# A decoder layer on one core: six raw panel buffers from the output projection on, and additions that read PSUM banks first at the end of a sweep's seven-product part

## The chip, the cores and the metric

The kernel runs on one core of one Trainium2 chip. The metric is the device time of one execution in microseconds (us); the median of several runs counts. TensorE (PE in the profile) multiplies, VectorE (DVE) and ScalarE (ACT) do elementwise work, GpSimd (POOL) builds some tables, and SyncE (SP) issues nearly all loads, in the order of its queue.

## The reference

One decoder layer over 256 tokens of width 2048, in float32 (`D_FF` is 8192). The first part mixes tokens (a causal pooling mixer beside RWKV-7 time mixing) and gives `mix`. The change touches what follows from `w_out` on, and the memory of the mixer's tables:

```python
mix = concatenate([pool_out, rwkv_out], -1)
x = x + mix @ w_out
h2 = rms_norm(x, mlp_norm)
x = x + square(relu(h2 @ w_ffn_up)) @ w_ffn_down
gate = sigmoid(rms_norm(x, ple_norm) @ w_ple_gate)
x = x + gate * (p @ w_ple_proj)
return rms_norm(x, final_norm)
```

## The kernel before

**Split operands.** Every float32 weight is used as the sum of a high half (`wh`, rounded to the matmul's type, made by ScalarE) and a low half (`wl`, the difference, made by VectorE). A product is three matmuls: high by high, low weight by high, high by low. Each matmul has 512 moving columns and one 128 by 128 stationary tile.

**Panels and rings.** Weights come from HBM in raw panels of 128 partitions by 1024 floats (512 KB), with one SP load each (`load_raw`, L146 to L149). Raw panels, `wh` and `wl` each have a ring of three buffers in the pool `wp`. A load can be issued when the last reader of the buffer's old panel is done, `wl` mostly.

**From the output projection on.** The half of `w_out`'s rows that the mixer leaves over is done at L1138 to L1140, in four column blocks of four panels each. The feed-forward network then runs in two halves. `ffn_half` computes 4096 hidden columns with `gemm_wide` (64 panels a half; lines L1102 and L1107 are its matmuls, L157 and L158 its splits) and then adds them back into the residual stream `xr` in two *down sweeps*, one for each 1024 output columns (`down_sweep`, `pair` 0 and 1).

**A down sweep** goes over 16 row blocks `kp`, of two raw panels each (`rx`, `ry`, tile `raw_d` in the profile). A plain row block has 8 products (24 matmuls). A row block in `SEVEN` uses Strassen's way with seven products (21 matmuls); VectorE forms four sums of raw panels for it (`td`, L1257 to L1260) and there are three `wl` for it instead of two. Matmuls stand at L1217 to L1219, the splits of the sweep at L1228 and L1229; `wl_d_7b` is the low half of the second panel of row block 7. In a seven-product row block the suffixes b, c and d are `ry` and the two pairs of sums, and `wad` is the split of half of `rx` (L1254). The halves with suffix d live in a pair of buffers of their own, tag `graw`.

**Banks.** Four banks take the plain products (`d_b`), two double banks `w16` and `w57` (`d_w`) take products 1, 6 and 5, 7. After the last row block of `seven` the four banks `b1`, `b6`, `b5`, `b7` are added into `xr` (L1273 to L1282): `add` is a VectorE instruction at L1237, `u` (tile `ud`) holds b1 + b6 and then also b7. The double banks have two buffers in all, which the next user waits for: the next sweep, the next half's `gemm_wide`, or the transposes `h3t` at L1124. The four plain banks are added at the end (L1285 to L1287).

**The last sweep** of the second half has only four seven-product row blocks, loads and splits eight panels of the gate's weights beside its own (`keep`, L1156 to L1165, also with buffers of tag `graw`), and starts transposing `xr` for the gate (`between`, `h3_part`). The gate and the projection of the per-layer embeddings follow, then the final norm.

**Order.** PE's order is written out by hand up to L1080. From there on, the order on every engine and of SP's queue is made by the framework's scheduler: it goes by program order, moved forward by the number in `tc.high_priority(...)` (20000 for splits, 30000 for the plain banks' additions), and by when it expects operands to be ready. On the chip each engine keeps that order.

**Memory.** The pools `const`, `wp` and `act` last for the whole kernel. The mixer's pool `rp` is closed at L1081 (`rctx.close()`), and `fp` takes its room. In the kernel before, the tables that only the mixer reads lie in `const`.

Of the kernel before, what the change touches and what calls it, by code (L numbers as in the profile page):

```python
# [9 lines left out]
F32 = mybir.dt.float32  # L10
F32R = mybir.dt.float32r
AF = mybir.ActivationFunctionType
ALU = mybir.AluOpType
# [3 lines left out]
T = 256  # L17
# [23 lines left out]
def trunk(  # L41
# [19 lines left out]
    nc = tc.nc  # L61
# [3 lines left out]
    act = ctx.enter_context(tc.tile_pool(name="act", bufs=1))  # L65
    psm = ctx.enter_context(tc.tile_pool(name="psm", bufs=4, space=PSUM))
    rctx = ctx.enter_context(ExitStack())
    psr = rctx.enter_context(tc.tile_pool(name="psr", bufs=4, space=PSUM))

    def mm_bank(name):  # L70
# [22 lines left out]
    nc.vector.memset(eps_g, GN_EPS)  # L93
    ident = const.tile([128, 128], F32, name="ident")
    make_identity(nc, ident)
    ones = const.tile([128, 128], F32, name="ones")
    nc.vector.memset(ones, 1.0)
    jsum = const.tile([128, 128], F32, name="jsum")
    cmask = const.tile([128, 128], F32, name="cmask")
    rmask = const.tile([128, T], F32, name="rmask")  # L100
    sbd = [const.tile([128, 4, 128], F32, name=f"sbd{i}") for i in range(2)]
    nc.gpsimd.memset(cmask, 0.0)
    for r0 in (0, 64):
        nc.gpsimd.memset(cmask[r0 : r0 + 64, r0 : r0 + 64], 1.0)
    nc.gpsimd.tensor_copy(jsum, cmask)
    cen = const.tile([128, 128], F32, name="cen")
    jhead = const.tile([128, 32], F32, name="jhead")
    nc.gpsimd.memset(jhead, 0.0)
    nc.gpsimd.tensor_copy(jhead[:, 0:2], cmask[:, ::64])
    for r0 in (0, 64):  # L110
# [3 lines left out]
    nc.gpsimd.memset(rmask.rearrange("p (c t) -> p c t", t=64)[:, :, 0:1], 0.0)  # L114
    for i in range(2):
        nc.vector.memset(sbd[i], 0.0)
    edge = const.tile([128, 4, 16], F32, name="edge")
# [6 lines left out]
    wband = const.tile([128, 4, 272], F32, name="wband")  # L124

    def make_bands():
        for g, win in enumerate(WINDOWS):
# [9 lines left out]
    omu = const.tile([128, m1 - m0], F32, name="omu")  # L137
    oka = const.tile([128, 8], F32, name="oka")

    def derived():  # L140
        ka0 = PARAM_COLS["k_a"]
# [1 line left out]
        nc.vector.tensor_scalar(oka, par_sb[:, ka0 : ka0 + 8], -1.0, 1.0, op0=ALU.mult, op1=ALU.add)  # L143
        nc.vector.scalar_tensor_tensor(cen, jsum, -1.0 / 64.0, ident, op0=ALU.mult, op1=ALU.add)

    def load_raw(src, n, name):  # L146
        raw = wp.tile([128, 1024], F32, tag="raw", name=f"raw_{name}")
        nc.sync.dma_start(raw[:, 0:n], src)
        return raw  # L149

# [166 lines left out]
    hsel = const.tile([128, 4, 128], F32R, name="hsel")  # L317
    nc.gpsimd.tensor_copy(hsel, hsel_f)

    def flat(t_):  # L320
# [122 lines left out]
    zf = const.tile([128, 3, T], F32, name="zf")  # L443
    zwa, zg, zg2 = zf[:, 0], zf[:, 1], zf[0:64, 2]

    def wag_out():
# [688 lines left out]
        return part, lambda k: hl[:, :, k, :]  # L1135

    h2_part, h2 = transposed("h2")
    for n in range(4):  # L1138
        run(gemm_toks(w_out[n], mix, f"o{n}", lambda banks: residual(banks, n), (6, 7, 2, 3)))
        h2_part("mlp_norm", n)  # L1140
# [54 lines left out]
    def down_sweep(hf, pair, ys, sboxes, hooks=(), between=None, seven=SEVEN):  # L1195

        nm = f"d{hf}{pair}"
        hooks = dict(hooks)
        b2, b4, b3, bx = (mm_bank(f"{nm}_b{i}") for i in range(4))
        w16, w57 = (wide_bank(f"{nm}_w{i}") for i in range(2))  # L1200
        b1, b6, b5, b7 = w16[:, 0], w16[:, 1], w57[:, 0], w57[:, 1]
        todo = {"2": 0, "3": 0, "4": 0, "x": 0, "1": 0, "5": 0, "6": 0, "7": 0}
        banks = {"2": b2, "3": b3, "4": b4, "x": bx, "1": b1, "5": b5, "6": b6, "7": b7}
        for kp in range(16):
            if kp in seven:
                for n in "1234567":
                    todo[n] += 1
            else:
                for n in "234x":
                    todo[n] += 2  # L1210
        left = dict(todo)

        def prod(n, a_, w_):
            first, last = left[n] == todo[n], left[n] == 1
            left[n] -= 1
            (ah, al), (wh, wl) = a_, w_
            nc.tensor.matmul(banks[n], ah, wh, start=first, stop=False)  # L1217
            nc.tensor.matmul(banks[n], ah, wl, start=False, stop=False)  # L1218
            nc.tensor.matmul(banks[n], al, wh, start=False, stop=last)  # L1219

        def halves_of(src, name, own=False):

            pool, kw = (fp, dict(bufs=2)) if own else (wp, {})
            wh = pool.tile([128, 1024], F32R, tag="graw" if own else "wh", name=f"wh_{name}", **kw)
            wl = pool.tile([128, 1024], F32R, tag="graw" if own else "wl", name=f"wl_{name}", **kw)
            with tc.high_priority(20000):
                for c in range(2):
                    nc.scalar.activation(wh[:, c * 512 : c * 512 + 512], src[:, c * 512 : c * 512 + 512], AF.Copy)  # L1228
                nc.vector.tensor_tensor(wl, src, wh.bitcast(F32), op=ALU.subtract)  # L1229
            return [(wh[:, c * 512 : c * 512 + 512], wl[:, c * 512 : c * 512 + 512]) for c in range(2)]  # L1230

        def xs(tt, c):
            o = pair * 1024 + c * 512
            return xr[tt][:, o : o + 512]

        def add(tt, c, src):
            nc.vector.scalar_tensor_tensor(xs(tt, c), src, s2[:, tt : tt + 1], xs(tt, c), op0=ALU.mult, op1=ALU.add)  # L1237

        for q, kp in enumerate((0, 2, 1, 4, 3, *range(5, 16)) if pair else range(16)):
            if q in hooks:  # L1240
                hooks[q]()
            y, j = ys[kp // 2], kp % 2 * 512
            a11, a21, a12, a22 = ((y[:, j + i * 128 : j + i * 128 + 128], y[:, 1024 + j + i * 128 : 1152 + j + i * 128]) for i in range(4))
            rx, ry = (load_raw(w_down[pair, hf * 32 + 2 * kp + i], 1024, f"{nm}_{kp}_{i}") for i in range(2))
            if kp in seven:
                i = SEVEN.index(kp)
                st = sboxes[kp][:, i % 2 * 1024 : i % 2 * 1024 + 1024]
                s1, s2_, s3, s4 = ((st[:, c * 128 : c * 128 + 128], st[:, 512 + c * 128 : 640 + c * 128]) for c in range(4))
                t_ = a8(1, f"t{nm}_{kp}")
                t1, t3, t2, t4 = (t_[:, c * 512 : c * 512 + 512] for c in range(4))  # L1250
                wa = fp.tile([128, 1024], F32R, tag="wa", name=f"wa{nm}_{kp}")
                w11 = wa[:, 0:512], wa[:, 512:1024]
                with tc.high_priority(20000):
                    split_sb(*w11, rx[:, 0:512])  # L1254
                w21, w22 = halves_of(ry, f"{nm}_{kp}b")
                with tc.high_priority(20000):
                    nc.vector.tensor_tensor(t1, rx[:, 512:1024], rx[:, 0:512], op=ALU.subtract)  # L1257
                    nc.vector.tensor_tensor(t3, ry[:, 512:1024], rx[:, 512:1024], op=ALU.subtract)
                    nc.vector.tensor_tensor(t2, t3, rx[:, 0:512], op=ALU.add)
# [12 lines left out]
            if kp == seven[-1]:  # L1272
                add(0, 0, b1)  # L1273
                u = fp.tile([128, 512], F32, tag="r", bufs=2, name=f"u{nm}")
                nc.scalar.activation(u, b1, AF.Copy)
                nc.vector.tensor_tensor(u, b6, u, op=ALU.add)
                add(0, 1, u)
                add(0, 1, b5)
                nc.vector.tensor_tensor(u, b7, u, op=ALU.add)
                add(1, 0, u)  # L1280
                add(1, 1, u)
                add(1, 1, b5)  # L1282
                if between is not None:
                    between()
        for n, tt, c in (("2", 0, 0), ("4", 1, 0), ("3", 0, 1), ("x", 1, 1)):  # L1285
            with tc.high_priority(30000):
                add(tt, c, banks[n])  # L1287
# [184 lines left out]
```

## Time and profile before

| what | value |
|---|---|
| median of three runs | 1193.17 us (1190.15 to 1196.21) |
| the profiled execution, its own time | 1191.21 us |
| its span | 1189.5 us |
| PE busy | 1169.6 us, 98% |
| DVE busy | 859.2 us, 72% |
| ACT busy | 702.5 us, 59% |
| DMA | 216.81 MB, mean 182 GB/s |
| granted clock of TensorE, mean | 0.998 |

The span is what the trace covers; the execution's own time is a little longer. All durations of single instructions below come from this one execution. In a row of the trace the first number is the start in us, the second the duration, then the engine, the line, the operation, and output and inputs by tile name; in brackets stands how long the engine was idle before it and what ended that. In a row of waits stand the total in us, the number of times and the longest.

### The profile page before, as it was taken

The numbers are of one execution on the slowest core, as the hardware profiler recorded it, in microseconds if no ns is written. First come the engines' busy times: TensorE is split into PE (matmuls) and PEld (weight loads), VectorE is DVE, ScalarE is ACT, GpSimd is POOL, SyncE is SP. The second block draws the span as 40 slices with busy tenths as digits, with TensorE's granted clock in tenths as the row PEclk, the third lists the DMA queues.
The fourth block names the chain that finished last, engine by engine and source line by source line (L and its number), as shares of the span: only waits on it lengthen the run. The fifth ranks groups of instructions, "written<-read, shape, count | busy, mean of one in ns | idle before, by whom it ended". The sixth has DMA issues, their size and how long they took to land.

```text
span 1189.5 us, 17244 instructions
## 1 busy us (share of the span) xinstructions
PE 1169.6 (98%) x6428; PEld 974.0 (82%) x6428; DVE 859.2 (72%) x1156; ACT 702.5 (59%) x1302; POOL 14.0 (1%) x73
## 2 busy tenths in 40 slices
PE   9999999999999999999999999999999999999997
PEld 8787777788887888888878788888888888778886
DVE  7696996955666666667778888666678788787543
ACT  8777858676445565545555564555555555568544
POOL 2100000000000000000000000000000000000000
PEclk9999999999999999999999999999999999999999
DMA  8454443354455565566556566655555665776631
GB/s 291 158 193 143 142 142 108 118 184 154 140 180 172 181 194 187 187 193 193 181 193 197 193 207 207 192 192 190 184 193 190 200 203 188 272 245 221 206 107 71
DMA packets 60756, 216.81 MB, mean 182 GB/s; under 512 B 6784, under 2 KB 7552, under 8 KB 60288
## 3 DMA queue, kind: packets, MB, share of 16 engines
q1 hardware_dynamic: 60240, 215.12, 55.0%
q8 instruction: 50, 0.82, 0.3%
q10 hardware_dynamic: 432, 0.60, 0.1%
q14 instruction: 34, 0.28, 0.1%
HBM read 213.59 MB, written 2.10 MB: 181 GB/s over the span
## 4 chain that ended last, share of the span: by engine, by line
PE 83%; DMA 6%; DVE 5%; ACT 3%; issue 2%; SPq 0%; POOL 0%; ACTq 0%; POOLq 0%; DVEq 0%
PE u_w L1102 20%; PE u_w L1107 10%; PE d_b L1218 5%; PE d_b L1219 5%; PE d_b L1217 4%; DMA raw_d<-in_w_ffn_down_dram 4%; PE gt_b L228 2%; PE gt_b L231 2%; PE gt_b L232 2%; PE zk_b L231 1%; PE zk_b L232 1%; PE o_b L231 1%; PE o_b L232 1%; PE zv_b L228 1%; PE o_b L228 1%
## 5 line engine op out<-in xcount | busy, mean ns | idle before, releaser
L1102 PE MATMUL u_w<-h,wh_u 128*128 128x512 f32 x1024 | 321.9, 395 | 0.0
L157 ACT ACTIVATE wh_u<-raw_u 128x512 fp32r<-128x512 f32 x256 | 147.5, 623 | 164.2 <-PE u_w L1102 101.6
L158 DVE TENSOR_TENSOR wl_u<-raw_u,wh_u 128x1024 fp32r<-128x1024 f32 x128 | 156.5, 1224 | 113.3 <-ACT wh_u L157 111.7
L1107 PEld LDWEIGHTS u_w<-h,wl_u 128*128 128x128 f32 x1024 | 192.3, 188 | 45.4
L1107 PE MATMUL u_w<-h,wl_u 128*128 128x256 f32 x1024 | 201.4, 278 | 0.0
L1102 PEld LDWEIGHTS u_w<-h,wh_u 128*128 128x128 f32 x1024 | 156.0, 189 | 0.1
L158 DVE TENSOR_TENSOR wl_gt<-raw_gt,wh_gt 128x1024 fp32r<-128x1024 f32 x24 | 29.4, 1224 | 24.1 <-ACT wh_gt L157 24.0
L157 ACT ACTIVATE wh_gt<-raw_gt 128x512 fp32r<-128x512 f32 x48 | 28.0, 641 | 22.8 <-PE gt_b L232 17.2
L1257 DVE TENSOR_TENSOR td<-raw_d 128x512 f32<-128x512 f32 x22 | 15.2, 692 | 32.6 <-DMA raw_d<-in_w_ffn_down_dram 32.6
L231 PE MATMUL gt_b<-wh_gt,h 128*128 128x512 f32 x96 | 37.3, 389 | 0.0
L232 PE MATMUL gt_b<-wh_gt,h 128*128 128x512 f32 x96 | 37.3, 389 | 0.0
L162 ACT ACTIVATE wad<-raw_d 128x512 fp32r<-128x512 f32 x22 | 13.9, 632 | 36.6 <-DMA raw_d<-in_w_ffn_down_dram 36.4
L158 DVE TENSOR_TENSOR wl_o<-raw_o,wh_o 128x1024 fp32r<-128x1024 f32 x16 | 19.6, 1223 | 12.9 <-ACT wh_o L157 11.4
L157 ACT ACTIVATE wh_o<-raw_o 128x512 fp32r<-128x512 f32 x32 | 18.4, 623 | 16.3 <-issue 6.9
L157 ACT ACTIVATE wh_zp<-raw_zp 128x512 fp32r<-128x512 f32 x32 | 18.6, 623 | 15.9 <-PE zp_b L232 7.2
L158 DVE TENSOR_TENSOR wl_zk<-raw_zk,wh_zk 128x1024 fp32r<-128x1024 f32 x16 | 19.4, 1222 | 9.9 <-ACT wh_zk L157 9.9
L231 PE MATMUL zv_b<-wh_zv,hTh 128*128 128x512 f32 x64 | 26.0, 406 | 0.0
L231 PE MATMUL zk_b<-wh_zk,hTh 128*128 128x512 f32 x64 | 25.2, 394 | 0.7 <-ACT wh_zk L157 0.7
L231 PE MATMUL zp_b<-wh_zp,hTh 128*128 128x512 f32 x64 | 25.7, 401 | 0.0
L228 PE MATMUL gt_b<-wl_gt,h 128*128 128x512 f32 x96 | 25.7, 389 | 0.0
L157 ACT ACTIVATE wh_zk<-raw_zk 128x512 fp32r<-128x512 f32 x32 | 18.4, 624 | 11.9 <-DMA raw_zk<-in_w_in_dram 5.7
L231 PE MATMUL zr_b<-wh_zr,hTh 128*128 128x512 f32 x64 | 25.4, 397 | 0.0
(809 smaller groups left out, 2966.1 us busy)
## 6 DMA issues: line engine op xcount, KB each, us to landing
raw_u<-in_w_ffn_up_dram SPq DMA_DIRECT2D x128, 512.0 KB, 3.5
raw_d<-in_w_ffn_down_dram SPq DMA_DIRECT2D x128, 512.0 KB, 4.2
raw_gt<-in_w_ple_gate_dram SPq DMA_DIRECT2D x24, 512.0 KB, 3.5
raw_zk<-in_w_in_dram SPq DMA_DIRECT2D x16, 512.0 KB, 3.8
raw_zr<-in_w_in_dram SPq DMA_DIRECT2D x16, 512.0 KB, 3.3
raw_zv<-in_w_in_dram SPq DMA_DIRECT2D x16, 512.0 KB, 3.4
raw_zp<-in_w_in_dram SPq DMA_DIRECT2D x16, 512.0 KB, 3.3
raw_o<-in_w_out_dram SPq DMA_DIRECT2D x16, 512.0 KB, 3.6
```

The lines of the kernel that those rows point to most:

```text
L157: nc.scalar.activation(wh[:, a * 512 : (a + 1) * 512], raw[:, a * 512 : (a + 1) * 512], AF.Copy)
L158: nc.vector.tensor_tensor(wl, raw, wh.bitcast(F32), op=ALU.subtract)
L162: nc.scalar.activation(h_ap, src_ap, AF.Copy)
L228: nc.tensor.matmul(banks[tt], ah[:, ts_], halves[a][1], start=False, stop=last)
L231: nc.tensor.matmul(banks[tt], ah[:, ts_], halves[a][0], start=i + a == 0, stop=False)
L232: nc.tensor.matmul(banks[tt], al[:, ts_], halves[a][0], start=False, stop=False)
L1102: nc.tensor.matmul(bank[:, ct, :].rearrange("p (s t) -> p s t", s=2), wh[:, cs[ct]], hl, start=k == 0, stop=False, skip_group_check=True,)
L1107: nc.tensor.matmul(bank[:, ct, 0:T], wl[:, cs[ct]], hl[:, 0, :], start=False, stop=k == 15, skip_group_check=True)
L1217: nc.tensor.matmul(banks[n], ah, wh, start=first, stop=False)
L1218: nc.tensor.matmul(banks[n], ah, wl, start=False, stop=False)
L1219: nc.tensor.matmul(banks[n], al, wh, start=False, stop=last)
L1257: nc.vector.tensor_tensor(t1, rx[:, 512:1024], rx[:, 0:512], op=ALU.subtract)
```

## The change

Two things are changed, and a third makes room for the first.

1. From the first `w_out` panel of L1138 on, `load_raw` counts its panels. From the fifth on, three panels in turn take buffers of a new ring of three in `fp` (tag `raw2`), and the next three take the old ring in `wp`. Each buffer is so used again after six panels.
2. In the additions after the seven-product part, the order is changed: `b5` is added to both places before `u` is. All instructions up to the last read of a bank are put at the splits' priority (20000); the last two, which read only `u`, stay at program order.
3. Tables that only the mixer reads (`ones`, `jsum`, `cmask`, `rmask`, `sbd`, `cen`, `jhead`, `edge`, `wband`, `omu`, `oka`, `hsel`, `zf`) move from `const` to a pool `mixc` that closes with the mixer.

```diff
+    mixc = rctx.enter_context(tc.tile_pool(name="mixc", bufs=1))
...
-    ones = const.tile([128, 128], F32, name="ones")
+    ones = mixc.tile([128, 128], F32, name="ones")
...
+    deep = []
+
     def load_raw(src, n, name):
-        raw = wp.tile([128, 1024], F32, tag="raw", name=f"raw_{name}")
+        own = False
+        if deep:
+            deep.append(name)
+            own = len(deep) > 5 and len(deep) % 6 < 3
+        if own:
+            raw = fp.tile([128, 1024], F32, tag="raw2", bufs=3, name=f"raw_{name}")
+        else:
+            raw = wp.tile([128, 1024], F32, tag="raw", name=f"raw_{name}")
         nc.sync.dma_start(raw[:, 0:n], src)
         return raw
...
     h2_part, h2 = transposed("h2")
+    deep.append("w_out")
     for n in range(4):
...
             if kp == seven[-1]:
-                add(0, 0, b1)
                 u = fp.tile([128, 512], F32, tag="r", bufs=2, name=f"u{nm}")
-                nc.scalar.activation(u, b1, AF.Copy)
-                nc.vector.tensor_tensor(u, b6, u, op=ALU.add)
-                add(0, 1, u)
-                add(0, 1, b5)
-                nc.vector.tensor_tensor(u, b7, u, op=ALU.add)
+                with tc.high_priority(20000):
+                    add(0, 0, b1)
+                    nc.scalar.activation(u, b1, AF.Copy)
+                    nc.vector.tensor_tensor(u, b6, u, op=ALU.add)
+                    add(0, 1, b5)
+                    add(1, 1, b5)
+                    add(0, 1, u)
+                    nc.vector.tensor_tensor(u, b7, u, op=ALU.add)
                 add(1, 0, u)
                 add(1, 1, u)
-                add(1, 1, b5)
                 if between is not None:
                     between()
```

More of the change, by code (lines that the diff above doesn't have):

```diff
@@ L95, in trunk @@
     make_identity(nc, ident)
-    ones = const.tile([128, 128], F32, name="ones")
+    ones = mixc.tile([128, 128], F32, name="ones")
     nc.vector.memset(ones, 1.0)
[L98 to L101, printed above, removed]
+    jsum = mixc.tile([128, 128], F32, name="jsum")
+    cmask = mixc.tile([128, 128], F32, name="cmask")
+    rmask = mixc.tile([128, T], F32, name="rmask")
+    sbd = [mixc.tile([128, 4, 128], F32, name=f"sbd{i}") for i in range(2)]
     nc.gpsimd.memset(cmask, 0.0)
@@ L105, in trunk @@
     nc.gpsimd.tensor_copy(jsum, cmask)
-    cen = const.tile([128, 128], F32, name="cen")
-    jhead = const.tile([128, 32], F32, name="jhead")
+    cen = mixc.tile([128, 128], F32, name="cen")
+    jhead = mixc.tile([128, 32], F32, name="jhead")
     nc.gpsimd.memset(jhead, 0.0)
@@ L116, in trunk @@
         nc.vector.memset(sbd[i], 0.0)
-    edge = const.tile([128, 4, 16], F32, name="edge")
+    edge = mixc.tile([128, 4, 16], F32, name="edge")
     nc.vector.memset(edge, 1.0)
@@ L121, in trunk @@
             nc.gpsimd.memset(edge[:, g, t : t + 1], float(win) / (t + 1))
-    wband = const.tile([128, 4, 272], F32, name="wband")
+    wband = mixc.tile([128, 4, 272], F32, name="wband")
     def make_bands():
@@ L136, in trunk @@
     m0, m1 = PARAM_COLS["mu_r"], PARAM_COLS["mu_wag"] + 3
-    omu = const.tile([128, m1 - m0], F32, name="omu")
-    oka = const.tile([128, 8], F32, name="oka")
+    omu = mixc.tile([128, m1 - m0], F32, name="omu")
+    oka = mixc.tile([128, 8], F32, name="oka")
     def derived():
@@ L316, in trunk @@
     nc.gpsimd.affine_select(hsel_f, hsel_f, [[-2048, 4], [-1, 128]], ALU.is_ge, 0.0, base=63, channel_multiplier=64)
-    hsel = const.tile([128, 4, 128], F32R, name="hsel")
+    hsel = mixc.tile([128, 4, 128], F32R, name="hsel")
     nc.gpsimd.tensor_copy(hsel, hsel_f)
@@ L441, in head_norm @@
         nc.vector.reciprocal(rs1, rs1)
-    zf = const.tile([128, 3, T], F32, name="zf")
+    zf = mixc.tile([128, 3, T], F32, name="zf")
     zwa, zg, zg2 = zf[:, 0], zf[:, 1], zf[0:64, 2]
```

## The prediction

> **What bounds the kernel now.** I read the page's engine rows first, which have TensorE (PE) busy nearly always, then a table of stretches for where it is not, then PE's waits, and only then single instructions. The table gives the length of each stretch, each engine's busy time in it, the granted clock and the DMA share.
>
> ```profile
> core 0: us, PE busy (x) PEld busy (x) DVE busy (x) ACT busy (x) POOL busy (x), PEclk, DMA share, GB/s
> ...
> 557.60:727.60 170.00, 168.19 (x735) 136.49 (x734) 141.67 (x160) 94.59 (x167) 0.00 (x0) 1.00 0.61 196
> 727.60:905.90 178.30, 178.30 (x1025) 155.54 (x1024) 119.67 (x145) 92.56 (x165) 0.00 (x0) 1.00 0.59 191
> 905.90:1080.20 174.30, 171.68 (x761) 139.69 (x759) 145.59 (x164) 103.66 (x186) 0.00 (x0) 1.00 0.67 222
> ```
>
> The reader is to see that in the second half's up-projection (727 to 905; the first half's is alike) PE is busy for every microsecond: deeper raw buffers can give nothing there. In the two stretches of down sweeps (557 to 727, 905 to 1080) PE has gaps. Everything the change can win lies in these 344 us. How much is that? A busy PE row hides part of a stall, because matmul ends are modelled, so I count by the spacing of starts.
>
> ```profile
> 690.81 0.39 PE L1217 MATMUL d_b<-wh_d_9a,y 128*128 128x512 f32 x1
> ...
> 696.25 0.39 PE L1217 MATMUL d_b<-wh_d_10a,y 128*128 128x512 f32 x1
> ...
> 682.81 0.39 PE L1217 MATMUL d_b<-wh_d_7b,y 128*128 128x512 f32 x1
> 683.40 0.50 PE L1218 MATMUL d_b<-wl_d_7b,y 128*128 128x512 f32 x1 [0.20 <-DVE wl_d_7b L1229]
> 683.73 0.40 PE L1219 MATMUL d_b<-wh_d_7b,y 128*128 128x512 f32 x1
> ...
> 1057.61 0.66 PE L1124 MATMUL h3t<-ident,x 128*128 128x128 f32 x4 [0.27 <-DVE ud L1276]
> 1058.02 0.48 PE L1219 MATMUL d_b<-wh_d_12a,y 128*128 128x512 f32 x1
> ```
>
> Panel row 9 is 24 matmuls in 696.25 − 690.81 = 5.44 us: 0.2267 us each without a stall. A sweep with six seven-product rows is 10 × 24 + 6 × 21 = 366 matmuls, the last sweep, with four, 12 × 24 + 4 × 21 = 372. The first pair would take 732 × 0.2267 = 165.9 us and takes 170.0: 4.1 lost. The second would take 738 × 0.2267 = 167.3 plus about twenty transposes at 0.41 / 4 each (2.1, from 1057.61 to 1058.02), and takes 174.3: 4.9 lost. So **9.0 us is the ceiling** of the whole change, 0.75% of the time. The Trainium skill, page "TensorE: Matmul & The Clock Gate", section "Wait — 56ns, not 53.3ns?", gives 215.7 ns as the warm start-to-start time for 512 columns; by it 1470 matmuls would hide another 16 us of loss in the sweeps. This trace shows 0.2267 in runs without any wait, so its spacing decides, and that 16 us is not there to win.
>
> The rows of 682.81 to 683.73 show what one stall costs: the next starts come 0.59 and 0.33 us later instead of 0.2267 each, 0.46 lost where the bracket says 0.20. A stall costs its idle time and 0.26 us. PE's other waits in the sweeps are these, beside the 0.27 of the h3t row at 1057.61:
>
> ```profile
> PE d_b L1218 <- DVE wl_d_8b L1229: 0.9, 1, 0.9
> PE h3t L1124 <- DVE x L1237: 0.7, 1, 0.7
> PE d_w L1218 <- DVE wl_d_6d L1229: 0.7, 1, 0.7
> PE d_b L1218 <- DVE wl_d_7b L1229: 0.6, 2, 0.4
> PE d_b L1218 <- DVE wl_d_6b L1229: 0.5, 1, 0.5
> PE d_b L1218 <- DVE wl_d_12b L1229: 0.3, 1, 0.3
> PE d_w L1218 <- DVE wl_d_6c L1229: 0.2, 1, 0.2
> PE d_b L1217 <- DVE x L1237: 0.2, 1, 0.2
> ```
>
> Seven stalls wait for a low half (wl) on DVE, three for additions. The chain of waits says why wl is late, for one of them:
>
> ```profile
> 590.04 4.28 DMA raw_d<-in_w_ffn_down_dram
> ...
> 594.96 1.15 ACT wh_d_7b L1228 x2
> ...
> 596.13 1.24 DVE wl_d_7b L1229
> ...
> 597.41 0.50 PE d_b L1218
> ```
>
> A raw panel must land (4.28), be rounded (1.15) and subtracted (1.24): 597.37 − 590.04 = 7.3 us with the gaps between. Only when its last reader is done does the buffer take the next load. Three buffers so give one panel per 2.4 us, with nothing to spare: PE eats two panels in 21 × 0.2267 or 24 × 0.2267 us, one per 2.4 to 2.7.
>
> ```profile
> SPq L148 <- DVE td L1259: 21.9, 12, 4.5
> ...
> DMA to landing us min/median/max: 3.3/4.2/6.9
> ...
> DVE td L1257 <- DMA raw_d<-in_w_ffn_down_dram: 32.6, 20, 3.6
> ```
>
> SyncE's queue waits for DVE to free a buffer, and DVE then sits idle for the panel that was asked for late.
>
> **The change part by part.**
>
> *Six buffers (A).* No instruction is added: the same loads on SP's queue, in runs of three to each pool. A load now waits for the panel six back, not three back, so it starts some three panels, 3 × 170 / 64 = 8.0 us, earlier, against 4.2 us of landing. The six stalls on wl_d_8b, 7b (two), 6b, 12b and 6c hang on a raw panel: 0.9 + 0.6 + 0.5 + 0.3 + 0.2 = 2.5 us idle, with 6 × 0.26 = 4.1 us lost. Bounds: nothing of it (DVE late by itself) and all of it. I take 3.7, near the top, because DVE has idle time to run ahead with (141.67 busy of 170). What is late next is DVE (priced under rival 3), and the wl and wh rings stay at three.
>
> *The stall on wl_d_6d (C)* has another cause.
>
> ```profile
> 1015.54 7.08 DMA graw<-in_w_ple_gate_dram
> ...
> 1025.09 1.24 DVE wl_d_6d L1229
> ...
> 1027.86 5.98 DMA raw_d<-in_w_ffn_down_dram
> ```
>
> wl_d_6d shares the graw pair with the kept gate panel, whose load took 7.08 us: the change leaves that pair alone. I cost it at no gain (0.7 + 0.26 stays). The load at 1027.86 stood in SP's queue behind the next graw load; with six buffers it can stand ahead of it, which is the 8b stall already counted in A.
>
> *Moved tables and SBUF.* Fourteen tiles of tables go to a pool that closes with the mixer; their writes and readers stay. The new ring lies where mixer tiles were, so its first load, the fifth of the output projection's second part, must wait for them. They are done long before: the mixer's last pool output stands at 318.43, and SP's eleven loads of that part run from 321.86 to 349.66.
>
> ```profile
> 318.43 0.48 DVE L987 SCALAR_TENSOR_TENSOR mp<-pm,par_sb,mp 128x256 fp32r<-128x256 f32 x1 [0.54 <-ACT mp L986]
> ...
> 321.86 27.80 SPq L148 DMA_DIRECT2D raw_o<-in_w_out_dram  x11
> ```
>
> Cost nothing; if it had to wait, one landing (4.2 us for raw_d) behind panels already split: 0 to 1 us.
>
> *Additions (B).* Same nine instructions per sweep, seven of them lifted to the splits' priority, reading b5 before the sums. Their bank pair w57 is free after the b7 read instead of two additions later.
>
> ```profile
> 629.25 1.22 DVE L1229 TENSOR_TENSOR wl_d_14a<-raw_d,wh_d_14a 128x1024 fp32r<-128x1024 f32 x1
> ...
> 632.78 0.74 DVE L1237 SCALAR_TENSOR_TENSOR x<-d_w,s2sq,x 128x512 f32<-128x512 f32 x1
> ...
> 634.58 0.68 DVE L1276 TENSOR_TENSOR ud<-d_w,ud 128x512 f32<-128x512 f32 x1
> ...
> 641.60 2.71 DVE L1237 SCALAR_TENSOR_TENSOR x<-d_b,s2sq,x 128x512 f32<-128x512 f32 x4
> ```
>
> Now they spread from 632.78 to 641.60, between splits, and end right ahead of the four additions that free the next sweep's banks. The three stalls on additions are 0.7 + 0.27 + 0.2 = 1.2 us idle, 2.0 us lost. Bounds: all 2.0 gone, or the adds delay splits (rival 1). I take 0.9, about half, since both stalled transposes still need the reads of b6 and b7, which come after their products. Behind the lifted additions on DVE stand wl_d_14a and its like, for which PE waits.
>
> Sum: 3.7 + 0.9 = **4.6 us off**. The profiled execution took 1191.21 us (span 1189.5), 1.96 under the median of 1193.17. On its own time that is 1186.6; on the median 1188.6.
>
> **The rivals.**
>
> *1, slower: lifted additions hold up a split.* DVE takes its instructions strictly in the order given:
>
> ```profile
> 581.00 1.15 ACT L1228 ACTIVATE wh_d_5b<-raw_d 128x512 fp32r<-128x512 f32 x2 [1.37 <-DVE wl_d_5a L1229]
> 584.48 0.69 DVE L1257 TENSOR_TENSOR td<-raw_d 128x512 f32<-128x512 f32 x1 [3.59 <-DMA raw_d<-in_w_ffn_down_dram]
> 585.09 1.22 DVE L1229 TENSOR_TENSOR wl_d_5b<-raw_d,wh_d_5b 128x1024 fp32r<-128x1024 f32 x1
> ...
> 630.35 0.39 PE L1219 MATMUL d_w<-wh_d_13d,S 128*128 128x512 f32 x1
> ...
> 631.49 0.39 PE L1218 MATMUL d_b<-wl_d_14a,y 128*128 128x512 f32 x1
> ```
>
> wl_d_5b was ready at 582.15 and stood 2.9 us behind a waiting td. The Trainium skill, page "Perfetto Trace Analysis", section "Tensor Engine Instruction (MATMUL, LD_WEIGHTS)", says the same of DVE, strict FIFO; the rows agree. If the additions come ahead of wl_d_14a, they wait for product 6 (630.35 + 0.39 = 630.74), then take 0.68 + 3 × 0.74 + 0.68 = 3.6, then the split 1.22: 635.5, where PE wants it at 631.49. That is 4.0 us at each of four sweep ends: 1188.6 + 16.0 = 1204.6; two ends make 1196.6. It decides from the second end on, and only where the split has not been issued before product 6 is done. Against it: before, that split ended at 630.47, and six buffers let it come earlier.
>
> *2, everything goes.* All 9.0 us lost in the sweeps vanish, also the 2 us that no wait row names: 1193.17 − 9.0 = 1184.2. For it: the up-projections, with a steady supply, have none. Against: the graw pair stays, and DVE has little room where a seven-product row and a plain one alternate (next rival).
>
> *3, nothing happens.* The raw ring was not the limit, the split rings of three are: DVE gets its panel early and cannot write. For it: a seven-product row costs DVE 5 × 0.69 + 3 × 1.22 = 7.1 us, a plain one 2.44, together 9.6 against 45 × 0.2267 = 10.2 on PE. Against: the 32.6 us in which DVE waited for raw_d at one line. Only B's 0.9 is left: 1192.3.
>
> **How the numbers follow.** Forecast 0.48 (its own range 1186.5 to 1191), rival 1 0.14, rival 2 0.26, rival 3 0.12. A measurement of this kernel tells about 0.5%, 6.0 us, from no change. Faster by more: all of rival 2 and 0.06 of the forecast, whose low end reaches past 6 us: 0.32. Slower by more: rival 1, whose likeliest forms hold up more than two ends, 0.14. The rest, 0.54, is within. The range 1183 to 1196 takes the ceiling with 1 us of scatter at the low end and rival 1 with not quite two ends at the high one; it leaves out some 0.15.
>
> **What would show it.** A right: SP's waits on td fall away, DVE's idle time on raw_d falls from 32.6 us to under 10, and the wl stalls of 7b, 8b, 12b, 6b are gone, with ACT waiting on PE instead. B right: no PE wait on x or ud at 642, 1057 and 1065, and additions in one block. C right: the stall on wl_d_6d stays. The prediction is wrong if the sweeps keep their 170 and 174 us, if new stalls stand on the split right behind the seven-product part, or if the time moves in the up-projections or the gate, where nothing waits now.

## The result, and the profile after

The changed kernel takes 1183.43 us in the median of six runs (1182.25 to 1184.84); the kernel before takes 1192.8 beside it (six runs, 1189.83 to 1196.21). The ratio is 0.9919, with a 95% interval of 0.9904 to 0.9935: 9.4 us faster. The forecast was 1188.6, or 4.6 us off, so the gain is twice the one that was forecast. 1183.43 lies below the forecast's own range (1186.5 to 1191), 0.4 us above the low end of the whole range (1183 to 1196), and at the number of rival 2 ("everything goes", 1184.2).

The profiled execution took 1184.84 us (span 1183.1), 6.4 less than the one of before (1191.21). From the starts of PE's instructions on the timeline I get the length of each stage. The two pairs of down sweeps went from 170.00 + 174.23 to 166.07 + 171.07, 7.1 us less. The projection of the per-layer embeddings, right behind the last sweep, gained 0.5; the gate, the two up-projections and the output projection's second part changed by less than 0.1. The stretch ahead of that part, which the change leaves as it was but for the place of its tables, was 1.3 us *longer* (331.66 against 330.32). It varies by itself: in a second profile of the changed kernel it took 330.48, and over all fourteen profiles of this case it lies between 329.9 and 332.0, with no order by what is changed. Four of them are above 331.6 and ten below 330.9. The four (the changed kernel's first, the additions alone, the second of the ring alone, and the last kernel below) are those in which the granted clock stands at 0.50 for some 3 us of this stretch, from 7.7 to 11.0 us or from 37.9 to 41.1; in the other ten it is 1.00 there. So these two profiles understate the gain by 1.3 us.

The table of stretches of the changed kernel (columns as before) shows PE busy without a gap in the first pair, and 1.0 us short of it in the second:

```profile
core 0: us, PE busy (x) PEld busy (x) DVE busy (x) ACT busy (x) POOL busy (x), PEclk, DMA share, GB/s
558.90:724.90 166.00, 166.00 (x734) 137.44 (x733) 138.22 (x156) 95.10 (x165) 0.00 (x0) 1.00 0.59 199
...
903.30:1074.30 171.00, 169.99 (x760) 140.34 (x759) 140.48 (x160) 103.47 (x185) 0.00 (x0) 1.00 0.65 222
```

Nearly the same work is done in less time: DVE is busy for 138 and 140 us, where it was for 142 and 146 with four more instructions in each stretch (1156 in the whole kernel, both times). Its waits, total, times and longest; the rows of SP are those of the first pair, and L1268 to L1271 are L1257 to L1260 of the kernel before:

```profile
PE h3t L1134 <- DVE h L1141: 1.0, 1, 1.0
...
DVE td L1269 <- DMA raw_d<-in_w_ffn_down_dram: 2.0, 5, 0.5
DVE td L1268 <- DMA raw_d<-in_w_ffn_down_dram: 2.0, 3, 0.8
...
SPq L158 <- DVE wl_d_7a L1240: 11.9, 2, 6.4
...
SPq L158 <- DVE td L1270: 5.6, 6, 1.3
...
SPq L158 <- DVE td L1271: 2.8, 2, 1.4
...
DMA to landing us min/median/max: 3.3/4.3/7.6
```

The first row is all that PE still waits for in the sweeps; ten stalls stood there before. DVE's idle time for raw panels is 4.0 us instead of 32.6 at one line alone. In the first pair the queue of SP waits for `td` for 8.4 us in 8 waits, where it was 38.4 us in 24. It still waits about as long in all (141 us, 146 before), now mostly for low halves, but for those of panels further back, and nobody downstream notices. A panel takes as long to land as before, 4.3 us against 4.2: it is only asked for earlier. From the load's issue to the first split that ScalarE makes of the panel, the median over the 128 panels of the sweeps is 12.7 us, 4.6 before, so 8.1 us earlier; the prediction had worked out 8.0.

### The profile page after: what moved, and what is told of

It reads as the page before. It is cut to its first block, busy times and chain, and to the rows that moved or that the text cites. A ratio compares the mean times of both kernels' runs of the same rounds, so it can differ in the third digit from the quotient of the medians.

```text
span 1183.1 us, 17263 instructions
## 1 busy us (share of the span) xinstructions
PE 1166.3 (99%) x6428; PEld 976.6 (83%) x6428; DVE 857.5 (72%) x1156; ACT 704.5 (60%) x1302; POOL 13.6 (1%) x73
## 4 chain that ended last, share of the span: by engine, by line
PE 95%; ACT 2%; DVE 1%; DMA 1%; issue 0%; POOL 0%; SPq 0%; ACTq 0%; POOLq 0%
PE u_w L1112 20%; PE u_w L1117 10%; PE d_b L1229 8%; PE d_b L1230 8%; PE d_b L1228 8%; PE gt_b L238 2%; PE gt_b L242 2%; PE gt_b L241 2%; PE d_w L1229 2%; PE d_w L1230 2%; PE d_w L1228 2%; PE zk_b L241 1%; PE zk_b L242 1%; PE o_b L241 1%; PE o_b L242 1%; PE zv_b L238 1%
## 5 line engine op out<-in xcount | busy, mean ns | idle before, releaser
L167 ACT ACTIVATE wh_zp<-raw_zp 128x512 fp32r<-128x512 f32 x32 | 18.6, 623 | 15.9 <-PE zp_b L242 5.7
L242 PE MATMUL zk_b<-wh_zk,hTl 128*128 128x512 f32 x64 | 25.6, 401 | 0.0
L168 DVE TENSOR_TENSOR wl_zv<-raw_zv,wh_zv 128x1024 fp32r<-128x1024 f32 x16 | 19.4, 1219 | 8.2 <-ACT wh_zv L167 7.3
L242 PE MATMUL zp_b<-wh_zp,hTl 128*128 128x512 f32 x64 | 25.0, 391 | 0.0
```

The lines of the kernel that those rows point to most:

```text
L167: nc.scalar.activation(wh[:, a * 512 : (a + 1) * 512], raw[:, a * 512 : (a + 1) * 512], AF.Copy)
L168: nc.vector.tensor_tensor(wl, raw, wh.bitcast(F32), op=ALU.subtract)
L242: nc.tensor.matmul(banks[tt], al[:, ts_], halves[a][0], start=False, stop=False)
```

## The experiments

Names of PE's and DVE's lines shift by a few between kernels; L1228 to L1230, L1240 and L1248 of the changed kernel are L1217 to L1219, L1229 and L1237 of the kernel before. Each kernel was run beside the kernel before on its chip, and that median is given with it. "Pair 1" and "pair 2" are the two pairs of down sweeps, by starts on PE as above.

### Which part gives what

**Ring alone**, with the old additions:

```diff
                 u = fp.tile([128, 512], F32, tag="r", bufs=2, name=f"u{nm}")
-                with tc.high_priority(20000):
-                    add(0, 0, b1)
-                    nc.scalar.activation(u, b1, AF.Copy)
-                    nc.vector.tensor_tensor(u, b6, u, op=ALU.add)
-                    add(0, 1, b5)
-                    add(1, 1, b5)
-                    add(0, 1, u)
-                    nc.vector.tensor_tensor(u, b7, u, op=ALU.add)
+                add(0, 0, b1)
+                nc.scalar.activation(u, b1, AF.Copy)
+                nc.vector.tensor_tensor(u, b6, u, op=ALU.add)
+                add(0, 1, u)
+                add(0, 1, b5)
+                nc.vector.tensor_tensor(u, b7, u, op=ALU.add)
                 add(1, 0, u)
                 add(1, 1, u)
+                add(1, 1, b5)
```

> The moved tables and the ring of six raw buffers, with the additions of the kernel before. Theory (the raw ring gives nearly all): the first pair of sweeps takes 166 to 167 us instead of 170.0, no wait on a low half (wl) is left on TensorE, the time is 7 to 9 us under before. Rival (the lifted additions give a good part): 4 to 6 us under before, with the three waits on x and ud of 1.2 us and their after-cost still there and the first pair at 167 or more.

1186.56 against 1194.22, ratio 0.9935 (0.9923 to 0.9947); pairs 166.92 + 174.04. PE's waits in its sweeps:

```profile
PE d_w L1229 <- DVE wl_d_6d L1240: 1.4, 1, 1.4
...
PE h3t L1134 <- DVE x L1248: 0.9, 2, 0.6
...
PE d_b L1228 <- ACT wh_d_2a L1239: 0.7, 1, 0.7
...
PE d_b L1228 <- DVE x L1248: 0.3, 1, 0.3
```

The ring clears the stalls on wl_d_6b, 7b, 8b, 12b and 6c by itself. The time and the first pair are as the theory had them, but a wait on a low half is left, against it, and so are the additions' waits, as the rival had it. What the ring leaves is of another kind: a wait for `wl_d_6d`, whose buffer pair the kept gate panels share, longer than before, waits on additions, and one of 0.7 at the first matmul of the last sweep. The view puts that one down to a split on ACT, but this matmul does not read that split; at the same matmul the second profile of this kernel, below, has a wait on `x`.

**Additions alone**, three raw buffers:

```diff
-    deep.append("w_out")
```

> The moved tables and the new additions, with three raw buffers as before. Theory (the raw ring gives nearly all): 0 to 1.5 us under before; the wl stalls stay. Rival of the prediction (lifted additions hold up a split where the supply is short): slower than before by 1 to 8 us, with a new stall of up to 4 us on the low half of the panel right behind the seven-product part.

1192.26 against 1194.22, ratio 0.9989 (0.9978 to 0.9999); pairs 170.88 + 174.88 in the profiled execution, at 1195.43 the longest of the eleven. PE's waits in its sweeps:

```profile
PE d_b L1228 <- DVE wl_d_7b L1239: 1.2, 2, 0.7
...
PE h3t L1134 <- DVE h L1141: 1.1, 1, 1.1
...
PE d_b L1228 <- DVE wl_d_8b L1239: 0.7, 1, 0.7
PE d_w L1228 <- DVE wl_d_6d L1239: 0.7, 1, 0.7
...
PE d_b L1228 <- DVE wl_d_6b L1239: 0.6, 1, 0.6
...
PE h3t L1134 <- DVE x L1247: 0.3, 1, 0.3
```

The stalls on late panels are still there; of the waits on `x` and `ud`, 1.1 us before (1.2 from rounded rows), 0.3 is left, and the transposes wait for 1.1 on an evacuation (`h`) instead. What rival 1 expected, a stall on the split right behind the seven-product part (`wl_d_14a`), does not appear.

**Tables alone**, with both of these edits:

> Only the tables move to the pool that closes with the mixer; three raw buffers and the additions as before. Theory: no change, within 2 us of before, the same stalls. Rival (where tiles lie in memory matters): the stretches before the up-projection change by 1 us or more.

1192.58 against 1194.22, ratio 0.9992 (0.9979 to 1.0006); pairs 169.20 + 176.08. The moved tables show neither a cost nor a gain clear of noise, and the additions alone are 0.3 us from them.

**Four raw buffers** instead of six, with the new additions:

```diff
-            own = len(deep) > 5 and len(deep) % 6 < 3
+            own = len(deep) > 5 and len(deep) % 4 == 2
...
-            raw = fp.tile([128, 1024], F32, tag="raw2", bufs=3, name=f"raw_{name}")
+            raw = fp.tile([128, 1024], F32, tag="raw2", bufs=1, name=f"raw_{name}")
```

> The whole change with a ring of four raw buffers in place of six (one buffer in the later pool). Theory (7.3 us from load to freed buffer, over four buffers 1.8 us a panel against the 2.4 to 2.7 that TensorE eats): most of the gain is there, 6 to 9 us under before, no wl stall on a raw panel. Rival (the loads must run ahead far enough to cover a whole seven-product row with its sums): 3 to 5 us under before, some of the wl stalls left.

1185.27 against 1193.05, ratio 0.9934 (0.9922 to 0.9947); pairs 166.06 + 171.65. One buffer more is enough for the first pair, to the tenth of a microsecond. By the 7.3 us that the prediction measured for one panel, from issue to split, four buffers give one per 1.8 us where PE takes one per 2.4 to 2.7; three gave one per 2.4. The median from issue to first split is 7.0 us here, 2.4 more than with three. Its one stall is again `wl_d_6d`, 1.1 us. The time is as the theory had it, 7.8 us under before.

### The additions on top of the ring

Ring alone and the whole change had not been run side by side. They were run again together on one chip, with a copy of the kernel before.

> The kernel before, profiled a second time. Its ordinary runs lie 2 to 3 us above the profiled execution of 1191.2. Theory (its panels arrive with nothing to spare, so every execution has other stalls on raw panels): the same stretches before the output projection and in the up-projections, but other or longer wl stalls in the sweeps and a total of the two pairs of sweeps over 344.2 us. Rival (the 2 to 3 us come from the mixer's start, which varies by itself): the two pairs within 0.5 us of 344.2 and the stretch up to the output projection longer.

> The whole change once more, beside the ring alone on the same chip. Theory (the lifted additions are worth something once the ring supplies): 1.5 to 4 us under the ring alone, no stall over 0.3 us but the one on the transposes' evacuation. Rival: within 1 us of the ring alone.

> The ring and the moved tables with the additions of before, once more, beside the whole change on the same chip. Theory: 6 to 8 us under before, with stalls on x, ud, the next sweep's first bank and wl_d_6d of 2 to 4 us together. Rival (the additions are worth nothing): the same time as the whole change.

Against 1192.6 for the kernel before, its copy took 1192.6 (ratio 0.9999, 0.9983 to 1.0016), the whole change 1182.65 (0.9924, 0.9908 to 0.994) and the ring alone 1187.8 (0.9964, 0.9951 to 0.9977). On one chip the additions bring 5.1 us on top of the ring, more than the 1.5 to 4 that were expected, while alone they brought 0.3 over the tables. The size is loose: by the ratios of the first runs (0.9935 for the ring, 0.9919 for the whole change) it is 1.9 us, and each ratio is known to 0.12 to 0.16%, or 1.4 to 1.9 us. Between the pairs in the two profiles of each of the two kernels it is 3.0 to 5.3. Stretches of the second pair, the whole change first, then the ring alone:

```profile
902.00:1071.70 169.70, 169.70 (x762) 140.46 (x760) 140.72 (x160) 103.66 (x185) 0.00 (x0) 1.00 0.66 224
```

```profile
904.00:1077.60 173.60, 171.05 (x761) 140.06 (x760) 141.74 (x160) 103.78 (x186) 0.00 (x0) 1.00 0.66 223
```

and PE's waits in the sweeps of the ring alone:

```profile
PE h3t L1134 <- DVE x L1248: 1.1, 2, 0.8
...
PE d_w L1229 <- DVE wl_d_6d L1240: 1.1, 1, 1.1
PE d_b L1228 <- DVE x L1248: 0.4, 1, 0.4
```

Here the changed kernel has no gap left at all in its sweeps, and the ring alone has four stalls of 2.6 us together. With 0.26 each on top that is 3.6, and its second pair was 3.8 us longer (173.49 against 169.66). Of the 3.6, 1.3 is the stall on `wl_d_6d`, which is not one on an addition (next section); 2.3 is left for the additions. DVE and PE of the ring alone, in the last sweep, show how the additions make a stall:

```profile
1051.91 0.74 DVE L1248 SCALAR_TENSOR_TENSOR x<-d_w,s2sq,x 128x512 f32<-128x512 f32 x1
...
1055.88 0.68 DVE L1290 TENSOR_TENSOR ud<-d_w,ud 128x512 f32<-128x512 f32 x1
...
1060.47 1.22 DVE L1240 TENSOR_TENSOR wl_d_14a<-raw_d,wh_d_14a 128x1024 fp32r<-128x1024 f32 x1 [1.06 <-ACT wh_d_14a L1239]
1061.61 0.74 DVE L1248 SCALAR_TENSOR_TENSOR x<-d_w,s2sq,x 128x512 f32<-128x512 f32 x1
...
1062.41 1.09 PE L1134 MATMUL h3t<-ident,x 128*128 128x128 f32 x8 [0.84 <-DVE x L1248]
```

The last addition that reads a bank (the second of `b5`) stands behind a split for which DVE idles 1.06 us; the bank comes free at 1061.61 + 0.74 = 1062.35, 10.4 us after the first addition, and the transposes stand waiting. In the kernel before these additions took as long at this place (10.7 us, 10.0 in its copy). Where they take longer with the ring is in the middle of a pair: 15.9 to 16.6 us there, 8.9 before. In the second profile of the whole change:

```profile
1047.38 1.40 DVE L1248 SCALAR_TENSOR_TENSOR x<-d_w,s2sq,x 128x512 f32<-128x512 f32 x2
...
1051.85 0.68 DVE L1292 TENSOR_TENSOR ud<-d_w,ud 128x512 f32<-128x512 f32 x1
...
1057.62 1.04 PE L1134 MATMUL h3t<-ident,x 128*128 128x128 f32 x8
```

All banks are read 5.2 us after the first addition (1052.53), and the transposes wait for nothing. In the first profile the banks were read as early, and the one wait of a transpose is that of 1.0 on `h`. Whether the order or the priority does it was not tried apart.

### The stall on wl_d_6d

The prediction said it stays, since the pair of buffers that it shares with the kept gate panels is not changed. It stayed with the ring (1.4, 1.1), and with four buffers and the new additions (1.1), and went in both profiles of the whole change. SP's and DVE's instructions around it, whole change:

```profile
1012.06 0.33 SPq L1170 DMA_DIRECT2D graw<-in_w_ple_gate_dram  x1
...
1014.59 0.60 SPq L1352 DMA_DIRECT2D fn<-in_final_norm_dram  x1
...
1018.64 1.23 DVE L1175 TENSOR_TENSOR gk<-graw,gk 128x1024 fp32r<-128x1024 f32 x1 [1.16 <-ACT gk L1174]
1019.90 1.23 DVE L1240 TENSOR_TENSOR wl_d_6d<-td,wh_d_6d 128x1024 fp32r<-128x1024 f32 x1
1021.05 1.22 DVE L1240 TENSOR_TENSOR wl_d_7a<-raw_d,wh_d_7a 128x1024 fp32r<-128x1024 f32 x1
```

and ring alone:

```profile
1019.83 1.23 DVE L1175 TENSOR_TENSOR gk<-graw,gk 128x1024 fp32r<-128x1024 f32 x1 [1.64 <-ACT gk L1174]
1020.97 1.22 DVE L1240 TENSOR_TENSOR wl_d_7a<-raw_d,wh_d_7a 128x1024 fp32r<-128x1024 f32 x1
1022.10 1.22 DVE L1240 TENSOR_TENSOR wl_d_6d<-td,wh_d_6d 128x1024 fp32r<-128x1024 f32 x1
```

With the ring, with or without the new additions, the kept panel is asked for ahead of the 1 MB of `fn` (ring alone: 1012.76 and 1015.39); before, `fn` came first. Counted from the start of the second pair, the whole change asks for it 1.0 to 1.3 us earlier than the ring alone. Its DVE also makes `wl_d_6d` ahead of `wl_d_7a`, one split of 1.13 us earlier; the kernel before has that order too, and the one with four buffers has not. All these are the scheduler's orders, moved by edits that do not name them. In every one of these kernels `wl_d_6d` comes behind the split of the kept panel (`gk`), the last reader of the buffer that it needs. To test the shared pair itself, the kept panels got a buffer of their own, on top of the ring alone:

```diff
-        raw = fp.tile([128, 1024], F32, tag="graw", bufs=2, name=f"graw{kp}")
+        raw = fp.tile([128, 1024], F32, tag="kraw", bufs=1, name=f"graw{kp}")
```

> The ring of six and the additions of before, and the kept gate panels load into a raw buffer of their own instead of the pair that the seven-product row's last halves use. Theory (wl_d_6d waits because it shares the pair with the kept panel): the stall of 1.35 us on wl_d_6d in the ring alone is gone, the time is 1 to 2 us under the ring alone (1186.6), and the last pair of sweeps takes 172.5 or less instead of 174.0. Rival (the stall is a matter of DVE's order of instructions, not of the pair): the stall stays or moves to the next split, no change.

1185.75 against 1193.05, ratio 0.9937 (0.9923 to 0.9951); pairs 167.20 + 171.92. The stall is gone, and pair 2 is 2.1 us shorter than with the ring alone in its first profile, 1.6 than in its second. DVE's order of `wl_d_6d` and `wl_d_7a` changed here too, but from the pair's start `wl_d_6d` is made 6.1 us earlier than in the ring alone (113.3 against 119.4), of which that order can give 1.13. So the shared pair is its cause. The medians do not settle the 1 to 2 us that were expected: 7.3 us under before, where the ring alone was 7.7 and 4.8. What is left are waits on `x` (1.3 us in three stalls) and one of 0.4 on an evacuation of `h3t`.

### Is the raw ring the limit, or the ring of splits?

Rival 3 said the split rings. So three raw buffers, old additions, and a fourth `wh` and `wl` for the sweeps:

```diff
+    turn = []
...
-            wh = pool.tile([128, 1024], F32R, tag="graw" if own else "wh", name=f"wh_{name}", **kw)
-            wl = pool.tile([128, 1024], F32R, tag="graw" if own else "wl", name=f"wl_{name}", **kw)
+            th, tl = ("graw", "graw") if own else ("wh", "wl")
+            if not own:
+                turn.append(name)
+                if len(turn) % 4 == 0:
+                    pool, kw, th, tl = fp, dict(bufs=1), "wh4", "wl4"
+            wh = pool.tile([128, 1024], F32R, tag=th, name=f"wh_{name}", **kw)
+            wl = pool.tile([128, 1024], F32R, tag=tl, name=f"wl_{name}", **kw)
```

> Three raw buffers and the additions as before, but four buffers each for the high and low halves within the sweeps (every fourth pair in the later pool). Theory (the limit is the time from a freed raw buffer to the next panel's split, 7.3 us over three buffers): the stalls on wl mostly stay, 0 to 3 us under before. Rival (the distance that the split rings allow is the limit): 5 to 9 us under before, like the whole change.

1189.98 against 1194.22, ratio 0.9965 (0.9952 to 0.9977); pairs 166.58 + 178.30. Neither theory has this. The first pair is cured as well as by six raw buffers. ACT still idles for raw panels, 73.5 us in the two pairs (80.0 before, 2.1 in the whole change); my reading is that the fourth split buffer gives the slack behind the split instead of ahead of it. The second pair is 4.1 us longer than before instead:

```profile
1022.01 0.39 PE L1229 MATMUL d_b<-wl_d_7a,y 128*128 128x512 f32 x1
1025.41 0.80 PE L1229 MATMUL d_w<-wl_d_6d,S 128*128 128x512 f32 x1 [3.01 <-DVE wl_d_6d L1245]
...
1026.42 0.63 PE L1229 MATMUL d_b<-wl_d_6d,y 128*128 128x512 f32 x1
1026.85 0.63 PE L1230 MATMUL d_b<-wh_d_6d,y 128*128 128x512 f32 x1
...
1031.50 0.39 PE L1228 MATMUL d_b<-wh_d_7b,y 128*128 128x512 f32 x1
```

The stall on the shared pair is 3.01 us, and behind it matmuls start 0.43 us apart until 1031.50. Two more runs took its causes away one by one. First the kept panels' own buffer (the diff above on top of this one):

> Three raw buffers, four buffers each for the high and low halves in the sweeps, the additions of before, and a raw buffer of its own for the kept gate panels. Theory (what counts is the distance from load to matmul, and more room at either place gives it; the 3.0 us stall on wl_d_6d and the slow matmuls after it came from the shared pair): 6 to 8 us under before, as with six raw buffers, last pair of sweeps 173 or less. Rival (only a deeper raw ring works): 3 to 5 us under before, new stalls on raw panels in the last pair.

1191.71 against 1193.05, ratio 0.9989 (0.9979 to 0.9998); pairs 166.96 + 177.61. The stall on wl_d_6d is gone, and one of 5.6 us stands at the transposes, on the bank that `ud` reads. The 6 to 8 us of the theory did not come, nor the rival's 3 to 5. So, the new additions on top:

> Three raw buffers, four buffers each for the halves in the sweeps, the kept panels' own raw buffer, and the new additions. Theory (with splits that run ahead, additions at program order come last on DVE and held the transposes by 5.6 us; lifted they do not): that stall is gone, 6 to 9 us under before, about as with six raw buffers. Rival (three raw buffers cannot do it whatever the additions): 1 to 4 us under before with stalls on raw panels in the last pair of sweeps.

1190.48 against 1192.6, ratio 0.9982 (0.9969 to 0.9995); pairs 166.58 + 179.28. The time is in the rival's range, and my theory that late additions held the bank fell: the stall is there with the early ones too.

```profile
1049.35 5.48 DMA raw_d<-in_w_ffn_down_dram
...
1054.93 1.15 ACT L1244 ACTIVATE wh_d_13b<-raw_d 128x512 fp32r<-128x512 f32 x2 [4.05 <-DMA raw_d<-in_w_ffn_down_dram]
1055.98 0.58 ACT L1292 ACTIVATE ud<-d_w 128x512 f32<-128x512 f32 x1
...
1056.59 0.69 DVE L1293 TENSOR_TENSOR ud<-d_w,ud 128x512 f32<-128x512 f32 x1 [2.48 <-ACT ud L1292]
...
1057.34 1.11 PE L1135 MATMUL h3t<-ident,x 128*128 128x128 f32 x4 [4.83 <-DVE ud L1293]
```

A raw panel is late; ACT idles 4.05 us for it, and the bank's copy stands behind that split in ACT's order. Its load was issued at 1049.35, when `wl_d_12a`, the low half of the panel three back, was done (1049.33). In the last sweep, with its extra loads, three raw buffers do not do, and a late panel now also holds banks.

### Is more to be had?

The whole change, the kept panels' own buffer, and the first two parts of `h3` evacuated at the splits' priority:

```diff
-                    nc.scalar.activation(h[:, j, :], src, AF.Copy, scale=col(norm, j))
...
+                    with tc.high_priority(20000 if ahead(n) else 0):
+                        nc.scalar.activation(h[:, j, :], src, AF.Copy, scale=col(norm, j))
...
-            h3_part, h3 = transposed("h3")
+            h3_part, h3 = transposed("h3", lambda n: n < 2)
```

> The whole change, with a raw buffer of their own for the kept gate panels, and with the evacuation of the first half of the last transposes at the splits' priority. Theory: the stall of 1.0 us of a transpose on the evacuation goes, the time is 1 to 2 us under the whole change (1183.4, ratio 0.9919). Rival (a stall there is only moved, since the split of panel 14 is then late): the same time within 1 us.

1183.84 against 1193.05, ratio 0.9924 (0.9912 to 0.9937); pairs 165.98 + 170.64, and PE's only wait for a line of the sweeps is 0.3 us on `x`. That is the change's own time, as the rival had it, though no stall was moved to panel 14. The two pairs stand 1.3 us above the floor of 335.3 that the prediction worked out, and those of the second profile of the change 0.3: there is next to nothing beyond it in this part of the kernel.

## Why the prediction was right, and where it was off

The direction and the cause of the larger part were right. The size was not: 4.6 us were forecast and 9.4 measured, and the likeliest of the three outcomes, no change beyond 6 us (0.54), did not come. That 1183.43 lies in the whole range is owed to rival 2, which set its low end, and in part to luck: it is inside by 0.4 us, and the second median of the changed kernel, 1182.65, is below it.

- *The ceiling of 9.0 us* held in the sweeps. In the second profile of the change the pairs take 165.98 + 169.66 = 335.64 us, 8.6 less than before, against the 335.3 worked out from 0.2267 us per matmul. The stalls that the prediction counted come to 4.1 (A), 2.0 (B) and 1.0 (C), 7.1 in all, and it took 3.7, 0.9 and nothing of them; it named the other 2 us only in rival 2.
- *Six buffers (A)*, taken at 3.7: right in the mechanism and about right in size. The ring alone is worth 3.3 us in the pairs by the first two profiles (344.23 to 340.96), although it made the stall on wl_d_6d longer by 0.7. Of the signs, three came true: DVE's wait on `raw_d` went from 32.6 to under 10, there is no stall on 6b, 7b, 8b, 12b or 6c, and ACT waits on PE instead (28.5 us in the two pairs before, 63.2 in the whole change; on raw panels 80.0 and 2.1). SP's waits on `td` fell to under a quarter but did not go. In medians, beside the kernel before, the ring alone is worth 4.8 and 7.7 us on two chips, above the 4.1 of the term's upper bound; what the rest is, the profiles do not show.
- *"The stall on wl_d_6d stays" (C)* was wrong. The cause was right (the kept panels' own buffer removes it), but I took the order of SP's and DVE's instructions as given, and it changed with the ring and again with the additions. That is 0.7 + 0.26 by the prediction's prices, 1.1 to 1.4 and 0.26 by the ring alone. It is luck as well: with four buffers and the same additions the scheduler made another order, and the stall stayed.
- *Moved tables*, nothing: right.
- *Additions (B)*, taken at 0.9 between bounds of 0 and 2.0: the term that was mis-sized. Alone they bring 0.3 us over the tables, on the ring 1.9 to 5.1, of which some 1.3 is the stall on `wl_d_6d`; their own stalls on the ring come to 2.3 us, a little above the upper bound. I halved them for a reason that did not hold: the stalled transposes do need the reads of b6 and b7, but with those lifted they wait on no addition. The bounds came from the waits of before, where late panels hid part of the additions' delay; with the ring the splits run ahead, the additions left at program order fall further behind in the middle of a pair (15.9 to 16.6 us from first to last bank, 8.9 before), and the price of leaving them there goes up. The waits on additions in the sweeps are 1.1, 0.6 and 0.7 us in the three profiles with rings of three and the old additions, and 1.8 (with the one of 0.7 above), 1.5 and 1.3 in the three with six. The effect of B hangs on A, and I summed the two; how much it grows stays open. Of the signs, "no PE wait on x or ud" came true in both profiles of the change; "in one block" did not, as a split (`wl_d_15a`) still stands between them.
- *Rival 1*, the lifted additions holding up a split, did not happen, alone or on the ring. DVE's rows of the whole change at the first pair's middle show why: the splits of row 14 are done before the first addition begins, and the next one stands between two of the lifted additions, none of which has to wait.

```profile
627.67 1.22 DVE L1240 TENSOR_TENSOR wl_d_14a<-raw_d,wh_d_14a 128x1024 fp32r<-128x1024 f32 x1 [1.48 <-ACT wh_d_14a L1239]
629.66 1.23 DVE L1240 TENSOR_TENSOR wl_d_14b<-raw_d,wh_d_14b 128x1024 fp32r<-128x1024 f32 x1 [0.77 <-ACT wh_d_14b L1239]
630.80 1.40 DVE L1248 SCALAR_TENSOR_TENSOR x<-d_w,s2sq,x 128x512 f32<-128x512 f32 x2
...
634.14 1.22 DVE L1240 TENSOR_TENSOR wl_d_15a<-raw_d,wh_d_15a 128x1024 fp32r<-128x1024 f32 x1
635.27 0.68 DVE L1292 TENSOR_TENSOR ud<-d_w,ud 128x512 f32<-128x512 f32 x1
```

- *Rival 2* has the size that came: 8.6 of the 9.0 us in the second profile, 7.1 in the first. It got 0.26. Of the arguments against it, DVE's little room held nothing up, and the graw pair did stay, but its stall went with the scheduler's order.
- *Rival 3* was half right: a fourth split buffer cures the first pair too. But DVE did not have its panels early; the ring of raw panels was short also. With the kept panels' own buffer, the last pair takes 177.6 us with four split and three raw buffers and 171.9 with six raw ones.

Left open: the median gain (9.4) is 3.0 us above the difference of the two profiles, and 1.3 of that is the longer opening of the profiled execution, with its half clock. The rest would fit stalls that differ from execution to execution: in the profile of the copy of the kernel before, the pairs took 343.2 us instead of 344.2, with one stall on 7b instead of two, and the six runs of the kernel before spread over 6.4 us, where the six of the change beside it spread over 2.6. But the copy's profile had been expected above 344.2 or within 0.5 of it, and it is neither, and runs without a profile show no stalls. So it is not shown.

## What to carry to other kernels

Count the time that a panel holds its buffer, from the load's issue to its last reader, and divide by the ring: that must be clearly shorter than the time in which TensorE eats a panel, not equal to it, and one buffer more than equality was enough here in the first pair, and nearly so in the last. When a change makes one supply earlier, price the next waits again under the new timing, because a cost that was hidden behind the old stall (bank-freeing additions at a low priority) can come out with it, and an edit that brings little alone can bring more on top of another. In a queue kept in order, put short instructions that free a bank ahead of splits that may wait for a load.

## What the runs showed of the hardware

A stall of 3 us costs more than its own time. The table of stretches around the stall of the kernel with four split buffers (PE alone; granted clock, DMA share, GB/s):

```profile
1022.40:1025.40 3.00, 0.00 (x0) 0.87 0.80 324
1025.40:1028.40 3.00, 2.99 (x7) 0.50 0.09 12
1028.40:1031.40 3.00, 3.00 (x8) 0.50 0.86 344
1031.40:1034.40 3.00, 3.00 (x14) 1.00 0.90 321
```

In 3.01 us without a matmul the granted clock fell to 0.50, and it took 6 us of matmuls at 0.43 us each to come back: 14 matmuls between 1025.41 and 1031.50, 6.09 us where 14 × 0.2267 = 3.2 would do, so 2.9 us on top of the stall. The stalls of 4.8 and 5.6 us in the next two kernels also ended at a clock of 0.50, with the same 0.43 us from start to start; none of the stalls up to 1.4 us in the sweeps did. The Trainium skill, page "TensorE: Matmul & The Clock Gate", section "HAM oscillation — how this bites in real kernels", gives gaps above about 3.4 us as the point from which the clock drops. Here 3.01 us was enough, or 3.40 from start to start. Less was enough in the opening of the kernel: in the second profile of the ring alone the clock stands at 0.50 from 37.9 to 41.1 us behind a wait of 1.14 us (1.62 from start to start). So these runs give no length of idle time from which it drops.
